# Three of four sums of weight halves moved from VectorE to GpSimd in a hybrid diffusion step

## The chip, the cores and the metric

The kernel runs on one core of a Trainium2 chip. A core has TensorE for matrix products (PE in the profile; PEld is its loading of weights), VectorE (DVE), ScalarE (ACT), GpSimd (POOL), and SyncE (SP), which starts DMA transfers. Each engine works through its own queue of instructions in order. The metric is the device time of one launch in microseconds. The kernel before was timed three times: 2074.26, 2075.63 and 2076.05 us, median 2075.63 us.

## The reference

One inference step through two layers, for 512 latent tokens and 128 context tokens (640 in all) with 1024 features, in float32:

```
h = RMSNorm(x) * (1 + scale1) + shift1            # modulation vectors: SiLU(cond) @ w_ada + b_ada
z = h @ w_in                                      # one projection for all branches, 6688 columns
A = gated linear attention (4 heads, both directions, chunks of 64)
B = short gated convolution;  C = Fourier mixing
x += gate1 * (sum_b sigmoid(G_b) * (branch_b @ W_b_out)) @ w_o
x += gate2 * (silu(g) * u) @ w_down,  with g, u = (RMSNorm(x) * (1 + scale2) + shift2) @ w_up
```

A final RMSNorm gives y_prompt and y_sample; the final attention states of the context are a third output.

## The kernel before

Features lie on the 128 partitions, tokens along the free axis, in two halves of 320 (256 latent and 64 context tokens). The products are made in float32 accuracy from two rounded parts: each operand is split into a high part (fp32r) and a low part, its difference from the high part, and three matmuls stand for one product (`mm3`, L224 to L226; `dense`, L242).

**Pairs of blocks.** Most of the projection (24 pairs of 128-column blocks in each layer, tiles `w1p_*`) and most of the up-projection (19 pairs in each layer, `wup_*`) are made two blocks at a time by the seven products of Strassen and Winograd (`pair`). That takes sums of halves of the weights and sums of the tokens' halves, and after the products four sums on the DVE that bring the seven results together in a tile `z`: L269, L271, L275 and L279, each with one operand in PSUM and one in SBUF. One pair has 84 matmuls of 320 columns.

**The weight stream.** Weights come by DMA into `raw` tiles (`_load`, six buffers; an SP transfer each). `_prep` turns them into chunks; a pair has four, called a, b, c and d. With r1 and r2 the two blocks' weights [128 x 1024] and a11, a12, a21, a22 their halves of 512 columns:

- chunk a is r1 itself;
- chunk b is `sb` = (a21 + a22 - a11, a11 - a21), with a21 + a22 kept as the first half of `sc`: L162, L163, L164;
- chunk c is `sc` = (a21 + a22, a12 - first half of `sb`): L168;
- chunk d is a22.

Each chunk is then split by `_split`: ScalarE copies it to `whi` (L140) and the DVE subtracts to get `wlo` (L141). `sb` and `sc` come from one pool with two buffers. `prefetch` prepares chunks up to two ahead of the one that TensorE takes.

**Around it.** In the mixer the heads of the attention run as generators beside the pairs: after certain products a step of the current head is issued (`tick_bg`). A head has, on the DVE, two scans (L617, L618), products with exponentials (L627 to L635), a serial chain of 14 small updates of the chunk states `S` (L667) and more; `S` shares its two buffers with the `z` tiles, and two memsets on GpSimd (L648, L649) clear parts of it. Modulation vectors (`ada`) come in between. In the feed-forward part the products down stand between the pairs up. GpSimd otherwise does a few transfers and memsets.

**The order.** The kernel is written in Tile: a planner lays out each engine's queue beforehand by priorities (the order of the program) and by its own idea of when operands and buffers are free, and puts in the waits. An engine's instructions can stand in another order than the program's text; on the chip an instruction that waits holds all behind it on its engine.

Of the kernel before, what the change touches and what calls it, by code (L numbers as in the profile page):

```python
# [16 lines left out]
PSUM = bass.MemoryType.PSUM  # L17
DRAM = bass.MemoryType.DRAM

P = 128  # L20
# [3 lines left out]
T = 640  # L24
TH = 320
# [21 lines left out]


def ffn_order():
    """The blocks of the second residual branch: those of one chunk's products down stand between the next's up."""  # L50
    todo = []
    for ci, (c0, n) in enumerate(FF_CHUNKS):
        for i in range(n):
            yield "up", ci, c0 + i
            for _ in range(-(-len(todo) // (n - i))):
                yield todo.pop(0)
        todo = [("down", ci, j) for j in range(KB)]


def ada_after(l, phase, i):  # L60
    """The quarters of modulation vectors made after the i-th block of a phase."""
    if phase == "mix":
        seq = [(l, v, n) for v in (G1, SH2, SC2, G2) for n in range(4)]
        return seq[i // 3 * 2 + i % 3 - 1:][:1] if i % 3 else []
    seq = [(1, v, n) for v in (SC1, SH1) for n in range(4)]
    return seq[i // 2 - 2:][:1] if l == 0 and i % 2 == 0 and 4 <= i < 20 else []
# [26 lines left out]
class Builder:  # L93
# [9 lines left out]
        self.n = 0  # L103
        self.gens, self.later, self.ada_last, self.last_act = [], [], None, None

# [1 line left out]
    def name(self, s):  # L107
        self.n += 1
        return f"{s}_{self.n}"
# [4 lines left out]
    def psum(self, s="ps"):  # L114
        return self.pp.tile([P, 1024], F32, tag="ps", name=self.name(s))

# [1 line left out]
    def start_stream(self, plan):  # L118
        self.plan = plan
        self.loads, self.chunks = [], []  # L120
# [23 lines left out]
    def _prep(self, c):  # L144
        nc = self.nc
        i, stage = self.chunks[c]
        if stage == "r":
            return
        if stage == "f":
            n = self.plan[i][2][0].shape[1]  # L150
            self.hl[c] = self._split(self.raw.pop((i, 0))[:, 0:n], n)
            self.freed += 1
            return
        r1, r2 = self.raw[i, 0], self.raw[i, 1]
        a11, a12, a21, a22 = r1[:, 0:512], r1[:, 512:1024], r2[:, 0:512], r2[:, 512:1024]
        if stage == "a":
            self.hl[c] = self._split(r1, 1024)
        elif stage == "b":
            sb = self.wp.tile([P, 1024], F32, tag="ws", name=self.name("sb"), bufs=2)
            sc = self.wp.tile([P, 1024], F32, tag="ws", name=self.name("sc"), bufs=2)  # L160
            self.sums[i] = sb, sc
            nc.vector.tensor_add(sc[:, 0:512], a21, a22)  # L162
            nc.vector.tensor_sub(sb[:, 0:512], sc[:, 0:512], a11)  # L163
            nc.vector.tensor_sub(sb[:, 512:1024], a11, a21)  # L164
            self.hl[c] = self._split(sb, 1024)
        elif stage == "c":
            sb, sc = self.sums.pop(i)
            nc.vector.tensor_sub(sc[:, 512:1024], a12, sb[:, 0:512])  # L168
            self.hl[c] = self._split(sc, 1024)
        else:  # L170
            self.hl[c] = self._split(a22, 512, True)
            del self.raw[i, 0], self.raw[i, 1]
            self.freed += 2
# [10 lines left out]
        return self.hl.pop(c)  # L184

    def prefetch(self, ahead):
        """Splits the weights that come next, up to some chunks ahead of the last taken."""
        self._load()
        while self.prepped < len(self.chunks):
            j = self.chunks[self.prepped][0]  # L190
            if sum(1 for q in range(self.used, self.prepped + 1) if self.chunks[q][1] != "d") > ahead:
                break
            if any((j, n) not in self.raw for n in range(len(self.plan[j][2]))):
                break
            self._prep(self.prepped)
            self.prepped += 1
            self._load()

# [1 line left out]
    def step(self, gens):  # L200
        for g in list(gens):
            try:
                next(g)
            except StopIteration:
                gens.remove(g)
# [12 lines left out]
        while self.gens:  # L218
            self.tick()

# [1 line left out]
    def mm3(self, o, lh, ll, rh, rl, start, stop):  # L222
        nc = self.nc
        nc.tensor.matmul(o, lh, rh, start=start, stop=False)  # L224
        nc.tensor.matmul(o, lh, rl, start=False, stop=False)  # L225
        nc.tensor.matmul(o, ll, rh, start=False, stop=stop)  # L226
# [16 lines left out]
        return ps  # L243

    def pair(self, key, h, T12, T34):
        """Two blocks of 128 columns over 8 blocks of the features and both halves of the tokens by the
        seven products of Strassen and Winograd; the two results, each [P, 2, TH]."""
        nc = self.nc

        def prod(o, w, c0, ops):  # L250
# [50 lines left out]
        self.nc.scalar.copy(hi, src)  # L301
        self.nc.vector.tensor_sub(lo, src, hi.bitcast(F32))

# [1 line left out]
    def consts(self):  # L305
        nc, cp, a = self.nc, self.cp, self.a
        self.ident = cp.tile([P, P], F32, name="ident")
# [27 lines left out]
            p["A2"] = cp.tile([P, KB, 2], F32, name=f"A2{l}")  # L335
            self.par.append(p)

# [1 line left out]
    def ada_mm(self, ps, kp, raw):  # L339
        r = raw.rearrange("p (k c) -> p k c", k=4)  # L340
        for j in range(4):
# [16 lines left out]
                nc.vector.scalar_tensor_tensor(p[A][:, ks], mv, 1.0, p[norm][:, ks], ALU.add, ALU.mult)  # L358

    def ada(self, pieces):  # L360
        """Quarters of modulation vectors; what follows the products comes one piece later."""
        for l, v, n in pieces:
            ps = self.psum("ada")
            for kp in range(2):
                self.ada_mm(ps, kp, self.take(("ada", l, v, n, kp)))
            self.ada_flush()
            self.ada_last = l, v, n, ps
# [3 lines left out]
            self.ada_end(*self.ada_last)  # L371
        self.ada_last = None

# [1 line left out]
    def table(self, name):  # L375
        """Loads a table set behind the functions of the one before."""
        self.in_order(lambda: self.tc.keep_in_program_order(self.nc.scalar.preload_act_table_set(name)))

    def act(self, *args, **kw):
        """A function that not all table sets have."""  # L380
        self.in_order(lambda: self.nc.scalar.activation(*args, **kw))  # L381

    def in_order(self, make):
# [40 lines left out]
        return r  # L424

    def modulate(self, half, r, xs, A, sh, out, hx):
        """Yields after each feature block's part of h."""
        nc = self.nc
        hs = slice(half * TH, half * TH + TH)

        def first(k):
            if len(hx) == k:
                hx.append(self.unit(s="hx"))
            nc.vector.tensor_mul(hx[k][:, hs], xs[k][:, hs], r)
            for i, (c0, n) in enumerate(((0, 256), (256, 64))):
                o = hx[k][:, half * TH + c0:half * TH + c0 + n]
                nc.scalar.activation(o, o, AF.Identity, scale=A[:, k, i:i + 1], bias=sh[:, k, i:i + 1])

        first(0)
        first(1)  # L440
        for k in range(KB):
            if k + 2 < KB:
                first(k + 2)
            if half == 0:
                out.append([])
            self.split_half(half, hx[k], out[k])
            yield
# [30 lines left out]
            self.nc.vector.scalar_tensor_tensor(o, ps[:, half * 512 + s:half * 512 + s + n], g[:, j, i:i + 1], o, ALU.mult, ALU.add)  # L478

    def boundary(self, keys, rhs, xs, g, after_x, norm, head, gk=None, tail=3):  # L480
        """The blocks that end a residual branch, the norm, and the blocks that start the next phase.

        The last few of the former and all of the latter go by halves of the tokens, so that the norm of
        one half runs beside the products of the other."""
        self.table("natural_log_exp_and_others")
        n = len(rhs)
        for j in range(KB - tail):
# [5 lines left out]
        last = range(KB - tail, KB)  # L493
# [50 lines left out]
            self.mm3h(ps, w, kb, self.hcur[kb], half, kb == 0, kb == KB - 1)  # L544

    def start(self, x, xs, A, sh, head):
        """The first norm and the first blocks, in the order in which the vectors come in."""
        nc = self.nc
        h, hx = [], []
        self.hcur, self.hx = h, hx  # L550
# [32 lines left out]
                    self.head_block(hps, hws, 0, k, half)  # L583
        return h, hx, hps

# [1 line left out]
    def to_tokens(self, u):  # L587
        """[P channels, T] to [P tokens, 5, P channels], in PSUM."""
        pt = self.psum("tt")
        for i in range(5):  # L590
            self.nc.tensor.transpose(pt[:, i * P:i * P + P], u[:, i * P:i * P + P], self.ident)
        return pt

# [1 line left out]
    def gla_start(self, l):  # L595
        nc = self.nc
        nc.gpsimd.tensor_scalar_mul(self.par[l]["nb_gk"], self.par[l]["b_gk"], -1.0)
# [99 lines left out]
        nc.vector.tensor_mul(yo, yo, r)  # L697
        yos[hd] = yo

# [1 line left out]
    def conv(self, l, j, sc, sx):  # L701
        nc = self.nc
        w = self.par[l]["conv_w"]
# [7 lines left out]
        nc.vector.scalar_tensor_tensor(cc[:, 4, 63:64], uc[:, 9, 0:1], w[:, 2, j:j + 1], cc[:, 4, 63:64], ALU.mult, ALU.add)  # L711
        return cv

# [1 line left out]
    def dft_load(self):  # L715
        out = []
        for i in range(2):
# [4 lines left out]
        return out  # L722

    def fourier(self, l, fxn, fr):
        """The Fourier mixing of both sequences. The even frequencies of the latent tokens come from the sums
        of the two halves of the positions, the odd ones from their differences."""
        nc = self.nc
        raw, d = self.dft_load(), []

# [82 lines left out]
            fr[g] = both(*u)  # L812
            yield

# [1 line left out]
    def make_plan(self):  # L816
        a = self.a
        plan = []
# [48 lines left out]
                full(("wd", l, ci, j), a["wd"][l, j][:, c0 * P:(c0 + n) * P])  # L867
        return plan

# [1 line left out]
    def gated(self, l, b, j, br, y, out):  # L871
        nc = self.nc
        nxt = BRANCHES.index(b) * KB + j + 2
# [198 lines left out]
    Builder(stack, tc, a).build()  # L1072


# [1 line left out]
def _blocks(w):  # L1076
    l, k, n = w.shape
    return np.ascontiguousarray(w.reshape(l, k // P, P, n // P, P).transpose(0, 3, 2, 1, 4).reshape(l, n // P, P, k))
# [80 lines left out]
```

## Time and profile before

| what | value |
|---|---|
| median of three runs | 2075.63 us |
| span of the profiled execution | 2075.0 us |
| TensorE busy | 2012.5 us, 97% |
| DVE busy | 1570.5 us, 76%, 2508 instructions |
| ScalarE busy | 919.4 us, 44% |
| GpSimd busy | 18.2 us, 1%, 52 instructions |
| mean granted clock of TensorE | 0.995 |

The profiled execution gives no time of its own beside its span; the span is 0.6 us below the median of the runs. A busy time counts the parts of the span in which an engine had an instruction under way. Matmuls are pipelined and overlap: one lasts some 0.31 us and the next starts 0.15 us later, so small gaps do not show in TensorE's busy time. The same holds on a smaller scale for the DVE, whose instructions start a little before the one ahead has ended.

### The profile page before, as it was taken

How to read it: one execution, taken by the hardware profiler on the slowest of the kernel's cores; microseconds unless marked ns; L12 is line 12 of the kernel's file. 1: busy time of each engine (PE TensorE's matmuls, PEld its weight loads, DVE VectorE, ACT ScalarE, POOL GpSimd, SP SyncE). 2: the span in 40 equal slices, each digit the busy share in tenths (PEclk: the TensorE clock that was granted, in tenths of full speed). 3: DMA queues.
4: the chain of work that ended last, by engine and by line, in shares of the span. 5: the costliest groups of instructions: out<-in, count | busy, mean ns of one | idle time of the engine just before them, and what ended most of it. 6: DMA issues, size and time to landing. Idle time of an engine off the chain costs nothing. (4 is left out here: it accounts for less than half of the span.)

```text
span 2075.0 us, 35216 instructions
## 1 busy us (share of the span) xinstructions
PE 2012.5 (97%) x14100; PEld 1936.3 (93%) x14100; DVE 1570.5 (76%) x2508; ACT 919.4 (44%) x1445; POOL 18.2 (1%) x52
## 2 busy tenths in 40 slices
PE   5999999999999999999999999999999999999997
PEld 2999998999999999999979999899999999999997
DVE  5778798877667777777677878898765787877876
ACT  5554435445445333333365454544543643333333
POOL 2000000000000000000000000000000000000000
PEclk9999999999999999999999999999999999999999
DMA  8254442554612333333232453335545222222222
GB/s 320 69 171 136 148 140 95 186 197 141 210 55 62 103 118 98 105 114 103 83 126 84 165 171 132 118 129 173 192 153 173 62 64 78 78 92 71 88 72 71
DMA packets 107139, 256.72 MB, mean 124 GB/s; under 512 B 13344, under 2 KB 46304, under 8 KB 106976
## 3 DMA queue, kind: packets, MB, share of 16 engines
q1 hardware_dynamic: 102528, 250.91, 36.8%
q8 instruction: 111, 1.82, 0.4%
q10 hardware_dynamic: 3728, 2.49, 0.4%
q0 software_dynamic: 720, 1.07, 0.1%
q14 instruction: 52, 0.43, 0.1%
HBM read 227.69 MB, written 26.74 MB: 123 GB/s over the span
## 5 line engine op out<-in xcount | busy, mean ns | idle before, releaser
L140 ACT CAST whi<-raw 128x1024 fp32r<-128x1024 f32 (+2 forms) x368 | 270.1, 734 | 529.5 <-PE wo L242 37.3
L141 DVE TENSOR_TENSOR wlo<-raw,whi 128x1024 fp32r<-128x1024 f32 (+2 forms) x368 | 304.4, 828 | 112.2 <-ACT whi L140 111.8
L242 PE MATMUL wd<-ffhi,whi 128*128 128x320 f32 x656 | 150.2, 310 | 0.0
L242 PE MATMUL wd<-fflo,whi 128*128 128x320 f32 x656 | 149.5, 309 | 0.0
L242 PE MATMUL wd<-ffhi,wlo 128*128 128x320 f32 x656 | 149.4, 309 | 0.0
L140 ACT CAST whi<-sb 128x1024 fp32r<-128x1024 f32 x86 | 90.3, 1050 | 125.7 <-PE wd L242 31.5
L140 ACT CAST whi<-sc 128x1024 fp32r<-128x1024 f32 x86 | 90.3, 1050 | 107.8 <-PE wd L242 48.0
L141 DVE TENSOR_TENSOR wlo<-sc,whi 128x1024 fp32r<-128x1024 f32 x86 | 104.9, 1220 | 30.2 <-ACT whi L140 29.6
L473 DVE SCALAR_TENSOR_TENSOR x<-wd,mod,x 128x512 f32<-128x512 f32 x212 | 106.7, 545 | 23.0 <-PE wd L242 23.0
L242 PEld LDWEIGHTS wd<-ffhi,whi 128*128 128x128 f32 x656 | 109.4, 188 | 3.3 <-ACT whi L140 3.3
L141 DVE TENSOR_TENSOR wlo<-sb,whi 128x1024 fp32r<-128x1024 f32 x86 | 104.8, 1219 | 6.8 <-ACT whi L140 6.7
L242 PEld LDWEIGHTS wd<-ffhi,wlo 128*128 128x128 f32 x656 | 109.7, 188 | 0.0
L242 PEld LDWEIGHTS wd<-fflo,whi 128*128 128x128 f32 x656 | 109.6, 188 | 0.0
L162 DVE TENSOR_TENSOR sc<-raw 128x512 f32<-128x512 f32 x86 | 59.3, 689 | 27.3 <-DMA raw<-in_w 26.0
L342 PE MATMUL ada<-raw,cond 128*32 128x256 f32 x768 | 56.5, 410 | 9.2 <-ACT cond L381 5.5
L163 DVE TENSOR_TENSOR sb<-sc,raw 128x512 f32<-128x512 f32 x86 | 59.1, 687 | 0.5
L168 DVE TENSOR_TENSOR sc<-raw,sb 128x512 f32<-128x512 f32 x86 | 59.1, 687 | 0.3
L242 PE MATMUL wb<-bhi,whi 128*128 128x320 f32 x256 | 59.2, 312 | 0.0
L164 DVE TENSOR_TENSOR sb<-raw,raw 128x512 f32<-128x512 f32 x86 | 59.0, 686 | 0.0
L242 PE MATMUL wb<-bhi,wlo 128*128 128x320 f32 x256 | 58.4, 309 | 0.0
L242 PE MATMUL wb<-blo,whi 128*128 128x320 f32 x256 | 58.3, 309 | 0.0
L342 PEld LDWEIGHTS ada<-raw,cond 128*32 128x32 f32 x768 | 20.8, 114 | 31.7 <-issue 7.2
(2254 smaller groups left out, 6417.0 us busy)
## 6 DMA issues: line engine op xcount, KB each, us to landing
raw<-in_w SPq DMA_DIRECT2D x104, 512.0 KB, 4.4
raw<-in_w_ada SPq DMA_DIRECT2D x96, 512.0 KB, 3.8
raw<-in_wu SPq DMA_DIRECT2D x88, 512.0 KB, 3.6
raw<-in_wd SPq DMA_DIRECT2D x96, 192.0 KB, 2.3
sgd<-z SPq DMA_DIRECT2D x48, 320.0 KB, 3.1
sgl<-sgd SPq DMA_DIRECT2D x48, 320.0 KB, 3.8
raw<-in_wb SPq DMA_DIRECT2D x48, 256.0 KB, 2.8
raw<-in_wo SPq DMA_DIRECT2D x16, 512.0 KB, 3.5
```

The source lines that it names most:

```text
L140: self.nc.scalar.copy(hi[:, 0:n], src)
L141: self.nc.vector.tensor_sub(lo[:, 0:n], src, hi[:, 0:n].bitcast(F32))
L162: nc.vector.tensor_add(sc[:, 0:512], a21, a22)
L163: nc.vector.tensor_sub(sb[:, 0:512], sc[:, 0:512], a11)
L164: nc.vector.tensor_sub(sb[:, 512:1024], a11, a21)
L168: nc.vector.tensor_sub(sc[:, 512:1024], a12, sb[:, 0:512])
L242: nc.tensor.matmul(o[h], w[:, sl], rhs[kb][h][part], start=(kb == 0 and first), stop=(kb == nk - 1 and last))
L342: self.nc.tensor.matmul(ps[32 * j:32 * j + 32, 0:256], self.cond[:, 4 * kp + j, :], r[:, j, :], start=(kp == 0), stop=(kp == 1))
L473: self.nc.vector.scalar_tensor_tensor(seg(xv), seg(v), g[:, j, i:i + 1], seg(xv), ALU.mult, ALU.add)
```

## The change

Three of the four sums are issued on GpSimd instead of the DVE: a21 + a22 and a11 - a21 of chunk b, and the second half of chunk c. The sum at L163 and all splits stay on the DVE. What is computed stays the same, operation for operation.

```
             self.sums[i] = sb, sc
-            nc.vector.tensor_add(sc[:, 0:512], a21, a22)
+            nc.gpsimd.tensor_add(sc[:, 0:512], a21, a22)
             nc.vector.tensor_sub(sb[:, 0:512], sc[:, 0:512], a11)
-            nc.vector.tensor_sub(sb[:, 512:1024], a11, a21)
+            nc.gpsimd.tensor_sub(sb[:, 512:1024], a11, a21)
             self.hl[c] = self._split(sb, 1024)
         elif stage == "c":
             sb, sc = self.sums.pop(i)
-            nc.vector.tensor_sub(sc[:, 512:1024], a12, sb[:, 0:512])
+            nc.gpsimd.tensor_sub(sc[:, 512:1024], a12, sb[:, 0:512])
             self.hl[c] = self._split(sc, 1024)
```

The rest of the diff takes out comments and docstrings; the line numbers stay.

## Rows read from the trace of the kernel before

**Rows 1.** The page: its first part (busy time of each engine, share of the span, instructions) and the DVE's line of its second part (busy share in tenths, 40 slices of 51.9 us).

```profile
PE 2012.5 (97%) x14100; PEld 1936.3 (93%) x14100; DVE 1570.5 (76%) x2508; ACT 919.4 (44%) x1445; POOL 18.2 (1%) x52
...
DVE  5778798877667777777677878898765787877876
```

**Rows 2.** Busy time of each engine in four stretches: the two mixers (70 to 470 us and 1085 to 1470 us) and the two feed-forward parts (680 to 1050 us and 1690 to 2045 us). Columns: the stretch, its length, then busy us and number of instructions of PE, PEld, DVE, ACT and POOL, the granted clock of TensorE, the share of the DMA engines, GB/s.

```profile
70.00:470.00 400.00, 392.09 (x2840) 372.41 (x2839) 324.80 (x503) 191.85 (x297) 3.66 (x13) 0.99 0.43 144
...
680.00:1050.00 370.00, 370.00 (x2592) 363.74 (x2591) 273.87 (x426) 132.37 (x189) 0.00 (x0) 1.00 0.34 109
...
1085.00:1470.00 385.00, 375.27 (x2738) 355.61 (x2740) 319.64 (x493) 186.61 (x284) 3.67 (x13) 1.00 0.43 142
...
1690.00:2045.00 355.00, 355.00 (x2423) 355.00 (x2422) 269.40 (x397) 127.86 (x178) 0.00 (x0) 1.00 0.26 78
```

**Rows 3.** What TensorE's matmuls waited for, over the whole span: the waiting tile and line, the releaser, total us, times, longest. L279 is the DVE's last sum of a pair of blocks.

```profile
PE w1p_17a L224 <- DVE z L279: 4.1, 2, 2.3
...
PE w1p_36a L224 <- DVE z L279: 2.9, 2, 1.5
...
PE w1p_44b L224 <- DVE z L279: 2.0, 2, 1.6
...
PE w1p_10a L224 <- DVE z L279: 0.5, 2, 0.3
```

**Rows 4.** The page's groups of instructions: two of the four sums, and the low part of the chunk that two of them feed. Columns: busy us, mean ns of one, then the DVE's idle time before them and what ended it.

```profile
L162 DVE TENSOR_TENSOR sc<-raw 128x512 f32<-128x512 f32 x86 | 59.3, 689 | 27.3 <-DMA raw<-in_w 26.0
...
L163 DVE TENSOR_TENSOR sb<-sc,raw 128x512 f32<-128x512 f32 x86 | 59.1, 687 | 0.5
...
L141 DVE TENSOR_TENSOR wlo<-sb,whi 128x1024 fp32r<-128x1024 f32 x86 | 104.8, 1219 | 6.8 <-ACT whi L140 6.7
```

**Rows 5.** The DVE's instructions in order of time in a crowded stretch of the second mixer: start us, duration us, line, tiles, shapes.

```profile
1275.89 0.69 DVE L162 TENSOR_TENSOR sc<-raw 128x512 f32<-128x512 f32 x1 [2.67 <-DMA raw<-in_w]
1276.50 0.68 DVE L164 TENSOR_TENSOR sb<-raw,raw 128x512 f32<-128x512 f32 x1
1277.10 0.68 DVE L163 TENSOR_TENSOR sb<-sc,raw 128x512 f32<-128x512 f32 x1
1277.71 0.83 DVE L616 TENSOR_TENSOR u<-u,u 128x640 f32<-128x640 f32 x1
```

**Rows 6.** GpSimd's groups of instructions: its widest write, the only two that read a tile, and the memsets of the state tile S with what ended GpSimd's idle time.

```profile
L603 POOL MEMSET zb<- 128x640 f32 x2 | 1.3, 640 | 1.7 <-DVE t L293 1.7
...
L597 POOL TENSOR_SCALAR nb_gk<-b_gk 128x4 f32<-128x4 f32 x2 | 0.5, 236 | 2.8 <-DMA b_gk<-in_b_gk 2.8
...
masks.py:199 POOL TENSOR_SCALAR_AFFINE_SELECT ident<-ident 128x128 f32<-128x128 f32 x1 | 0.3, 309 | 0.1
...
L648 POOL MEMSET S<- 64x128 f32 x8 | 1.6, 199 | 529.9 <-DVE wlo L141 192.7 <-DMA sgd<-z 137.2 <-DVE sb L163 71.6
```

**Rows 7.** In order of time, one memset on GpSimd and two of the DVE's sums beside it (start us, duration us).

```profile
1101.05 0.64 POOL L599 MEMSET scanm<- 128x640 f32 x1 [751.13 <-DVE tlo L302]
...
1101.17 0.49 DVE L291 TENSOR_TENSOR t<-hx,hx 128x320 f32<-128x320 f32 x1
1101.57 0.49 DVE L292 TENSOR_TENSOR t<-hx,t 128x320 f32<-128x320 f32 x1
```

**Rows 8.** Busy time of the DVE in the second mixer (1085 to 1470 us) by source line, in this order: L162, L164, L168, L269, L271, L275, L279. Columns: the stretch, its length, busy us and number of instructions.

```profile
1085.00:1470.00 385.00, 15.87 (x23) 1.00 0.43 142
...
1085.00:1470.00 385.00, 15.78 (x23) 1.00 0.43 142
...
1085.00:1470.00 385.00, 15.80 (x23) 1.00 0.43 142
...
1085.00:1470.00 385.00, 19.66 (x24) 1.00 0.43 142
...
1085.00:1470.00 385.00, 11.72 (x24) 1.00 0.43 142
...
1085.00:1470.00 385.00, 19.70 (x24) 1.00 0.43 142
...
1085.00:1470.00 385.00, 19.42 (x24) 1.00 0.43 142
```

**Rows 9.** The DVE's instructions in order of time ahead of a wait of TensorE in the second mixer.

```profile
1176.87 0.68 DVE L168 TENSOR_TENSOR sc<-raw,sb 128x512 f32<-128x512 f32 x1
...
1179.40 0.69 DVE L162 TENSOR_TENSOR sc<-raw 128x512 f32<-128x512 f32 x1
...
1180.01 1.93 DVE L667 SCALAR_TENSOR_TENSOR S<-S,g 64x128 f32<-64x128 f32 x5
...
1183.23 2.63 DVE L667 SCALAR_TENSOR_TENSOR S<-S,g 64x128 f32<-64x128 f32 x7
...
1185.90 1.23 DVE L141 TENSOR_TENSOR wlo<-sc,whi 128x1024 fp32r<-128x1024 f32 x1
...
1187.54 0.82 DVE L279 TENSOR_TENSOR z<-w1p_34d,z 128x640 f32<-128x640 f32 x1
```

**Rows 10.** Two stretches of 25 us of the first mixer; columns as in rows 2.

```profile
275.00:300.00 25.00, 22.73 (x172) 21.44 (x171) 22.03 (x38) 9.55 (x19) 0.40 (x2) 0.93 0.40 137
...
325.00:350.00 25.00, 23.10 (x157) 22.08 (x156) 24.04 (x39) 9.31 (x16) 0.40 (x2) 0.93 0.22 63
```

## The prediction, made before the result was known

> **What bounds the kernel now.** I read the page's busy times first. TensorE is busy in 97% of the span, the DVE in 76%, GpSimd in 1% [rows 1]. Of the 2075.0 us only 62.5 are free of matmuls, so nothing that is done to the DVE can bring more than part of that. The busy times by stretch say where the free time lies [rows 2]: in the two feed-forward parts TensorE is busy in 370.00 of 370 us and in 355.00 of 355 us, so there the DVE, at 274 and 269 us, costs nothing. In the two mixers TensorE is free for 400 - 392.1 = 7.9 us and 385 - 375.3 = 9.7 us, 17.6 us together, while the DVE is busy for 81% and 83%. The other 45 us lie at the start, at the two ends of residual branches and at the end, where no pair is made. The list of waits names the releaser in the mixers [rows 3]: TensorE waits for the DVE's last sum of a pair (L279) for 4.1 + 2.9 + 2.0 + 0.5 = 9.5 us, in eight places, four in each layer. These 9.5 us are what a lighter DVE can win and what a heavier one makes larger.
>
> How such a wait comes about is seen in order of time [rows 9]: between 1176.87 and 1188.36 us the DVE has two of the sums, the chain of 14 updates of S, splits, and only then the L279 that frees the PSUM tile. The whole queue is late, not one instruction.
>
> **What is removed.** One of the sums lasts 0.69 us [rows 4], but in a crowded stretch the next starts 0.60 us after it (1275.89, 1276.50, 1277.10, 1277.71) [rows 5]. So a pair gives back 3 x 0.60 = 1.8 us of the DVE's queue; over 86 pairs that is 155 us. In the second mixer's stretch there are 23 such sums of each kind [rows 8], so 23 x 1.8 = 41 us of 385.
>
> **What is added.** GpSimd gets the same three instructions for each pair. The trace has no sum of two tiles on GpSimd. Bounds of its duration at 512 columns: from below the widest memset, 640 ns for 640 columns, scaled to 0.51 us; from above the one operation over a whole tile that reads a tile, 309 ns for 128 columns [rows 6], times four for the columns and twice for the second operand, 2.5 us. I take 4 x 0.309 = 1.24 us, as the nearest row reads, computes and writes. Then GpSimd is busy for 23 x 3 x 1.24 = 86 us of 385, and with the upper bound for 170 us: it does not become the bound by its own time.
>
> **What GpSimd costs the DVE** is the term that decides. From below: nothing. Beside a memset at 1101.05 the DVE's sums at 1101.17 and 1101.57 last 0.49 us each and keep their 0.40 us spacing [rows 7]; but a memset reads nothing. From above: the DVE stands still for the whole of each GpSimd sum, 86 us against the 41 removed. I take the middle case, that only those DVE instructions stand still that read two operands from SBUF, as GpSimd's sums do, and that instructions with an operand in PSUM go on. In the second mixer the DVE has 319.6 us [rows 2]; less the three sums (15.87 + 15.78 + 15.80 = 47.5) and the four sums behind the products (19.66 + 11.72 + 19.70 + 19.42 = 70.5) [rows 8] that leaves 201.7 us, 52% of 385. A GpSimd sum that falls anywhere then costs the DVE 0.52 x 1.24 = 0.65 us, and 69 of them cost 45 us, against 41 us removed. The DVE gains nothing and loses nothing. With 0.51 us for one the DVE gains 41 - 18 = 23 us, with 2.5 us it loses 90 - 41 = 49 us of the 65 us that it is free now; both ends stay in the range.
>
> The Trainium skill has a rule for this ("SBUF — State Buffer", section "Who interferes with whom"): a DVE instruction with two inputs in SBUF contends with a GpSimd instruction that reads SBUF, not with one that only writes, and whichever comes second waits until the first is done. The memset row agrees with its second half, and no run here yet shows the first. Without the rule, by the memset row alone, the sum would be the first rival's 2066 us; by the rule it is the 52% above.
>
> The Trainium skill also prices such a sum ("GPSIMD Engine Reference", section "Performance versus the Vector engine"): 1.96 times the DVE's time for the same sum. On the DVE's 0.69 us that is an estimate of 1.35 us, by which the 45 us would be 48 us; the sum of the forecast would not move.
>
> **What moves in the queues.** The sum that stays (L163) now waits at the head of the DVE's queue for GpSimd's first sum. Behind it stand splits and the sums after the products, so a late GpSimd would hold all of them, and then TensorE. But the first sum needs only the raw weights and a free buffer, and GpSimd's queue has nothing else than a few memsets, so it starts as soon as it may, often long before the DVE reaches L163: L162 stands at 1179.40, ahead of the chain of S [rows 9]. The wait for weights that the DVE had at L162, 26 us in all [rows 4], moves to GpSimd, and to L163 behind it. Where weights come that late, L163 ends 1.24 + 0.60 us after them and the three sums ended 1.8 us after them: equal. ScalarE's copy of `sb` waits for GpSimd's second sum in the same way. In GpSimd's queue the memsets of S (L648) wait for a buffer that a transfer or the DVE must free [rows 6]; sums behind such a memset wait too. No transfer is issued on another queue than before; SP's loads keep their order. The planner lays out the queues anew for the lighter DVE; which instruction goes ahead of which there can move single waits of 1 to 2 us either way.
>
> **The sum.** Feed-forward parts: nothing, because TensorE has no gap there to fill, and even the upper case (18 pairs x 3 x 1.24 - 18 x 1.8 = +35 us on 274) leaves the DVE at 309 of 370 us. Mixers: the DVE's load stays the same, so the 9.5 us of waits stay. Span 2075.0 + 0; with the 0.6 us that the median lies above the profiled span, 2075.6, I say 2075.5 us. Its own range is 2072 to 2079, for the waits that a new order shifts.
>
> **Rivals.**
>
> 1. *GpSimd's sums cost the DVE nothing, and the waits go.* Then each of the eight waits is shortened by up to the 1.8 us that leave the queue ahead of it. The two at w1p_17a (up to 2.3) lose 1.8 each, the two at w1p_36a their 2.9 us, those at w1p_44b and w1p_10a their 2.5 us: 9.0 us, 2066 us. Two stretches of the first mixer have a mean granted clock of 0.93 after such waits [rows 10]; if those dips went too, 2 x 0.07 x 25 = 3.5 us more. Range 2062 to 2071. For it speaks that the waits are the DVE's own; against it that GpSimd's sums, unlike its memsets, read two tiles.
>
> 2. *The DVE is held where it is already late: slower.* In the stretch ahead of a wait [rows 9] the queue holds the chain of S (64 partitions, two operands in SBUF) and splits, hardly anything with PSUM. Two GpSimd sums become free to run there, as the splits release their buffers, and each holds the DVE for the whole of its 1.24 us: 2.5 us against the 1.2 us of L168 and L162 that leave. Each of the eight heads' waits grows by 1.3 us, 10 us in all: 2086 us, and with dips of the clock as in rows 10 behind longer waits up to 2096. It decides as soon as the held share there is over 1.2 / 2.5 = 48%, if nothing else makes room. Against it: six of the fifteen slices that lie in the mixers have the DVE at 7 tenths [rows 1], so it can recover between heads.
>
> 3. *GpSimd is late.* Memsets of S that wait, or sums that themselves wait for the DVE, make L163 stand at the head of the DVE's queue for up to one GpSimd sum. With one such wait of 1.24 us for each of four heads in a layer that reaches TensorE, half of it hidden: 8 x 0.6 = 5 us, 2080 us.
>
> 4. *The change doesn't do what it says*, for instance if GpSimd refused to run beside the DVE at all: the DVE's 86 - 41 = +45 us in each mixer would leave it 92 to 95% busy there; the time is that of rival 2 at its upper end.
>
> **How the numbers follow.** A measurement of this kernel can tell 0.2%, 4.2 us, from no change: 2071.5 to 2079.8. I give the forecast 0.40, the first rival 0.32, the second with the fourth 0.20, the third 0.08. Most of the forecast's cases lie within 0.2%, and a few of the first rival's smallest gains fall there too, against a few of the forecast's that leave it: same 0.39, faster 0.32, slower 0.29 (0.20 + 0.05 of the third and 0.04 of the forecast's upper edge). The range for 8 in 10 reaches to the first rival's lower part and to the second's middle: 2063 to 2088.
>
> **What would show it.** In the profile after: the duration of L162, L164 and L168 on GpSimd (1.24 us; over 2 or under 0.8 moves the sum); the mean of the DVE's L141 and L163, which now stand at 1.22 and 0.69 us: longer if GpSimd holds the DVE, unchanged if not; L279 beside it should not lengthen. The DVE's busy time in 1085 to 1470 us: about 320 by the forecast, 278 by the first rival, over 335 by the second. TensorE's waits for L279: 9.5 us by the forecast, under 2 by the first rival, near 20 by the second. A wait of L163 for GpSimd in the DVE's list, over 20 us, would be the third. The forecast is wrong if TensorE's free time in the mixers leaves 14 to 21 us, or if the feed-forward parts change at all.

## The result, and the profile after

The changed kernel takes 2105.25 us (median of four runs, 2104.44 to 2107.64) against 2075.84 us of the kernel before beside it. The ratio is 1.0146, with a 95% interval of 1.0132 to 1.0160: slower by 1.5%, some 30 us. The forecast was 2075.5 us with a range of 2063 to 2088. The profiled execution has a span of 2103.3 us, 28.3 us more than before. One execution each of e3 and e5 below (2814 and 2202 us) ran at a much lower granted clock, 0.66 and 0.85, and is left out of their medians and ratios.

First the page of the changed kernel: the busy times, and the groups of the sums and of one split (columns as in [rows 4]).

```profile
PE 2024.4 (96%) x14100; PEld 1947.7 (93%) x14100; DVE 1544.0 (73%) x2250; ACT 919.2 (44%) x1445; POOL 410.3 (20%) x310
...
L162 POOL TENSOR_TENSOR sc<-raw 128x512 f32<-128x512 f32 x86 | 122.0, 1419 | 1335.1 <-DVE wlo L141 533.7
...
L164 POOL TENSOR_TENSOR sb<-raw,raw 128x512 f32<-128x512 f32 x86 | 128.5, 1494 | 177.0 <-DVE wlo L141 168.9
...
L168 POOL TENSOR_TENSOR sc<-raw,sb 128x512 f32<-128x512 f32 x86 | 143.1, 1664 | 96.9 <-DVE sb L163 96.3
...
L163 DVE TENSOR_TENSOR sb<-sc,raw 128x512 f32<-128x512 f32 x86 | 120.7, 1403 | 49.5 <-POOL sc L162 46.9
...
L141 DVE TENSOR_TENSOR wlo<-sc,whi 128x1024 fp32r<-128x1024 f32 x86 | 113.1, 1315 | 36.0 <-ACT whi L140 35.7
```

The DVE has 258 instructions less, but its busy time falls only from 1570.5 to 1544.0 us. The three sums that left were worth 3 x 59 = 177 us of it by their own durations and about 155 us by their spacing. The rest is found again as longer durations: L163, untouched by the change, goes from 0.687 [rows 4] to 1.403 us, 62 us over the 86 pairs, and the split of `sc` from 1.220 to 1.315 us; smaller amounts lie in other splits and in the DVE's work for the heads and the convolution. The sums behind the products, which have one operand in PSUM (where the matmuls put their results; the other tiles lie in SBUF), are not longer: the second mixer's 24 of L269 take 19.56 us against 19.66 before [rows 8]. On GpSimd a sum takes 1.42 to 1.66 us in the mean; the shortest of them take 1.26 us.

Where the 28.3 us lie: the next rows cover, for each kernel, the pairs of the two mixers, from the first pair's first product to the last pair's d product (columns as in [rows 2]; in the second mixer both ends are 1.3 us later within those products). Before:

```profile
78.20:447.10 368.90, 360.99 (x2615) 342.11 (x2614) 303.98 (x468) 176.40 (x269) 3.66 (x13) 0.99 0.43 143
...
1098.90:1467.00 368.10, 358.37 (x2616) 339.15 (x2615) 305.51 (x470) 176.17 (x269) 3.67 (x13) 1.00 0.43 144
```

After:

```profile
77.50:456.40 378.90, 364.31 (x2617) 344.75 (x2616) 296.25 (x402) 176.76 (x269) 110.48 (x81) 0.98 0.42 139
...
1112.20:1492.70 380.50, 364.18 (x2616) 344.69 (x2615) 299.90 (x403) 176.71 (x270) 109.95 (x81) 0.98 0.42 139
```

The two stretches grow by 10.0 and 12.4 us. TensorE's free time in them goes from 7.9 + 9.7 = 17.6 to 14.6 + 16.3 = 30.9 us, +13.3 us. The other 9.1 us are in its busy time, with 2615 to 2617 matmuls in each of the four: the granted clock falls from 0.99 and 1.00 to 0.98 in both. In stretches of 25 us, those with a mean granted clock of 0.93 were two, both in the first mixer [rows 10]; now there are eight in the two mixers, two of which are:

```profile
1300.00:1325.00 25.00, 23.00 (x156) 21.95 (x156) 22.03 (x29) 9.03 (x14) 9.22 (x6) 0.93 0.47 157
...
1400.00:1425.00 25.00, 24.73 (x186) 23.64 (x187) 20.77 (x41) 8.43 (x18) 6.18 (x4) 0.93 0.42 146
```

Each such stretch has 7% of 25 us, 1.75 us, less of the full clock, so six more of them account for 10.5 us, near the 9.1. Note the DVE: it is *less* busy than before in these stretches (296.2 and 299.9 against 304.0 and 305.5 us).

The feed-forward parts, which [rows 2] showed without a gap, still have none:

```profile
667.00:1030.00 363.00, 363.00 (x2544) 356.75 (x2544) 266.59 (x367) 130.60 (x188) 73.79 (x53) 1.00 0.32 100
...
1704.00:2055.00 351.00, 351.00 (x2396) 351.00 (x2395) 259.33 (x345) 126.21 (x177) 76.92 (x53) 1.00 0.27 81
```

Of the remaining 5.9 us, 5.4 are at the ends of the first residual branches, where the first pairs of the feed-forward part are prepared: from the first matmul of `wo` to the first pair it takes 107.1 instead of 104.2 us and 106.8 instead of 104.3 us. TensorE's busy time has 1.6 and 1.2 us of that, in stretches where the granted clock is lower than before (0.98 against 1.00).

What TensorE waited for after, the largest that the DVE's sums of a pair release (against the four rows of [rows 3]):

```profile
PE u L653 <- DVE z L269: 8.1, 4, 2.7
...
PE w1p_48d L224 <- DVE z L269: 4.2, 2, 2.2
...
PE w1p_36a L224 <- DVE z L279: 3.4, 2, 2.3
...
PE w1p_40d L224 <- DVE z L269: 2.5, 2, 1.3
...
PE w1p_44b L224 <- DVE z L279: 2.3, 2, 1.9
...
PE w1p_17a L224 <- DVE z L279: 1.3, 2, 0.7
```

L279 is still there with 3.4 + 2.3 + 1.3 us, but most is now L269, the *first* sum of a pair, which stood in no such row before. (`u` is a product of an attention head; it needs the PSUM tile that L269 frees.) In the DVE's own queue, L163 waits for GpSimd:

```profile
DVE sb L163 <- POOL sc L162: 46.9, 16, 5.8
```

The order of time at one late pair of the first mixer shows both together. Before, on the DVE:

```profile
151.77 0.69 DVE L162 TENSOR_TENSOR sc<-raw 128x512 f32<-128x512 f32 x1 [3.66 <-DMA raw<-in_w]
...
152.98 0.69 DVE L163 TENSOR_TENSOR sb<-sc,raw 128x512 f32<-128x512 f32 x1
...
153.58 1.22 DVE L141 TENSOR_TENSOR wlo<-raw,whi 128x1024 fp32r<-128x1024 f32 x1
...
154.71 0.82 DVE L269 TENSOR_TENSOR z<-w1p_34b,s 128x640 f32<-128x640 f32 x1
```

After, GpSimd, then the DVE, then TensorE and the clock of TensorE just behind (columns as in [rows 2]):

```profile
152.94 1.30 POOL L162 TENSOR_TENSOR sc<-raw 128x512 f32<-128x512 f32 x1 [11.26 <-DMA raw<-in_w]
...
154.20 1.29 POOL L164 TENSOR_TENSOR sb<-raw,raw 128x512 f32<-128x512 f32 x1
...
156.12 2.18 POOL L168 TENSOR_TENSOR sc<-raw,sb 128x512 f32<-128x512 f32 x1 [0.63 <-DVE sb L163]
```

```profile
154.27 1.77 DVE L163 TENSOR_TENSOR sb<-sc,raw 128x512 f32<-128x512 f32 x1 [5.75 <-POOL sc L162]
...
155.96 1.21 DVE L141 TENSOR_TENSOR wlo<-raw,whi 128x1024 fp32r<-128x1024 f32 x1
...
157.10 0.81 DVE L269 TENSOR_TENSOR z<-w1p_34b,s 128x640 f32<-128x640 f32 x1
```

```profile
157.97 1.53 PE L653 MATMUL u<-v,koT 64*128 64x128 f32 x18 [1.88 <-DVE z L269]
```

```profile
159.20:162.40 3.20, 3.20 (x13) 2.98 (x12) 2.99 (x6) 2.45 (x10) 1.27 (x1) 0.50 0.45 164
```

Before, the first sum starts when the weights are there (151.77) and L269 starts 2.94 us later. After, GpSimd starts its first sum at 152.94. L163 waits for it until 154.27, and in the same moment GpSimd starts its second sum (154.20). L163 lasts 1.77 us instead of 0.69: it ends when the second sum has ended (155.49) and its own 0.6 us are over. L269 starts 4.16 us after the first sum did, 1.2 us later than before. The third sum at 156.12 lasts 2.18 us: this time the DVE's split (155.96 to 157.17) was first. TensorE waits 1.88 us for L269, where before it went through the same products without a wait, and behind the wait the granted clock is 0.50, the lower of its two levels (1.2 instead of 2.4 GHz). Late weights are not the reason in general: measured against the matmuls at the same place of TensorE's queue, the 104 loads of `w_in` land 0.3 us earlier than before in the mean.

The smallest example is an instruction of four columns. Beside a GpSimd sum from 115.22 to 116.52, the DVE's sum L355 (0.16 us on its own) lasts until just that end:

```profile
115.22 1.30 POOL L162 TENSOR_TENSOR sc<-raw 128x512 f32<-128x512 f32 x1
```

```profile
115.56 0.97 DVE L355 TENSOR_TENSOR mod<-mod,b_ada 128x4 f32<-128x4 f32 x1
```

### The profile page after: what moved, and what is told of

It reads as the page before. It is cut to its first block, busy times and chain, and to the rows that moved or that the text cites. A ratio compares the mean times of both kernels' runs of the same rounds, so it can differ in the third digit from the quotient of the medians.

```text
span 2103.3 us, 35457 instructions
## 1 busy us (share of the span) xinstructions
PE 2024.4 (96%) x14100; PEld 1947.7 (93%) x14100; DVE 1544.0 (73%) x2250; ACT 919.2 (44%) x1445; POOL 410.3 (20%) x310
## 5 line engine op out<-in xcount | busy, mean ns | idle before, releaser
L141 DVE TENSOR_TENSOR wlo<-raw,whi 128x1024 fp32r<-128x1024 f32 (+2 forms) x368 | 323.9, 881 | 120.7 <-ACT whi L140 120.1
L162 POOL TENSOR_TENSOR sc<-raw 128x512 f32<-128x512 f32 x86 | 122.0, 1419 | 1335.1 <-DVE wlo L141 533.7
L164 POOL TENSOR_TENSOR sb<-raw,raw 128x512 f32<-128x512 f32 x86 | 128.5, 1494 | 177.0 <-DVE wlo L141 168.9
L168 POOL TENSOR_TENSOR sc<-raw,sb 128x512 f32<-128x512 f32 x86 | 143.1, 1664 | 96.9 <-DVE sb L163 96.3
L163 DVE TENSOR_TENSOR sb<-sc,raw 128x512 f32<-128x512 f32 x86 | 120.7, 1403 | 49.5 <-POOL sc L162 46.9
L140 ACT CAST whi<-sc 128x1024 fp32r<-128x1024 f32 x86 | 90.3, 1050 | 136.4 <-PE wd L242 48.0
L141 DVE TENSOR_TENSOR wlo<-sc,whi 128x1024 fp32r<-128x1024 f32 x86 | 113.1, 1315 | 36.0 <-ACT whi L140 35.7
```

The lines of the kernel that those rows point to most:

```text
L140: self.nc.scalar.copy(hi[:, 0:n], src)
L141: self.nc.vector.tensor_sub(lo[:, 0:n], src, hi[:, 0:n].bitcast(F32))
L162: nc.gpsimd.tensor_add(sc[:, 0:512], a21, a22)
L164: nc.gpsimd.tensor_sub(sb[:, 512:1024], a11, a21)
L168: nc.gpsimd.tensor_sub(sc[:, 512:1024], a12, sb[:, 0:512])
```

## The experiments

Three theories stood against each other. **Held**: a GpSimd instruction that reads SBUF stops the DVE's instructions with two operands in SBUF for its whole length. **Wait**: the cost is the DVE's new wait at L163 for a slower engine. **Order**: the cost is the planner's new order of the queues. Ratios below are each against runs of the kernel before on the same chip, with 95% intervals.

**Nothing read (e1).**

```
-            nc.gpsimd.tensor_add(sc[:, 0:512], a21, a22)
+            nc.gpsimd.memset(sc[:, 0:512], 0.01)
...
-            nc.gpsimd.tensor_sub(sb[:, 512:1024], a11, a21)
+            nc.gpsimd.memset(sb[:, 512:1024], 0.01)
...
-            nc.gpsimd.tensor_sub(sc[:, 512:1024], a12, sb[:, 0:512])
+            nc.gpsimd.memset(sc[:, 512:1024], 0.01)
```

> The three sums on GpSimd are replaced by memsets of the same three tile halves, so these sums are left out and the output is not the reference's. Same engine, same wait of L163 for GpSimd, but nothing read from SBUF. Theory 'held' (a GpSimd instruction that reads SBUF stops the DVE's two-operand instructions for its whole length): L163 back to 0.69 us, L141 at its old means, TensorE free for under 12 us in the two mixers, 2062 to 2070 us. Theory 'order' (the planner's new queues cost the time): above 2090 us. Theory 'wait' (L163 waiting for another engine costs the time): 2080 us or more.

2061.77 us, ratio 0.9931 (0.9916 to 0.9945): 14 us faster than before. Busy times, two groups of the DVE and one of GpSimd:

```profile
PE 2006.6 (97%) x14100; PEld 1933.5 (94%) x14100; DVE 1423.8 (69%) x2250; ACT 920.0 (45%) x1445; POOL 148.2 (7%) x310
...
L163 DVE TENSOR_TENSOR sb<-sc,raw 128x512 f32<-128x512 f32 x86 | 59.2, 688 | 3.1
...
L141 DVE TENSOR_TENSOR wlo<-sc,whi 128x1024 fp32r<-128x1024 f32 x86 | 105.0, 1220 | 44.9 <-ACT whi L140 44.5
...
L162 POOL MEMSET sc<- 128x512 f32 x86 | 45.3, 526 | 1531.8 <-DVE wlo L141 1483.3 <-DVE mod L355 48.5
```

Every duration of the DVE in these groups is back at its old value, and its busy time falls by 147 us, near the 155 us that the forecast set for the three sums. TensorE is free for 10.1 us in the mixers (4.6 + 5.4), under the 12 expected. The DVE's queue in the mixers stands in the changed kernel's order but for single neighbours that swap. So the planner's order is not the cause: nearly the same queues run in 2062 us if GpSimd only writes. But a memset needs no weights and is done early, so the wait of L163 did not stay as expected: the DVE's list has none for GpSimd. This run takes away the reading and the lateness together, and shows what the first rival would have been worth; the next one parts them.

**The wait kept, nothing read (e9).**

```
-            nc.gpsimd.tensor_add(sc[:, 0:512], a21, a22)
-            nc.vector.tensor_sub(sb[:, 0:512], sc[:, 0:512], a11)
-            nc.gpsimd.tensor_sub(sb[:, 512:1024], a11, a21)
+            for t in (a21, a21, a21): nc.gpsimd.memset(t, 0.01)
+            nc.vector.tensor_sub(sb[:, 0:512], a21, a11)
+            for t in (sb[:, 512:1024], sb[:, 512:1024], sc[:, 0:512]): nc.gpsimd.memset(t, 0.01)
...
-            nc.gpsimd.tensor_sub(sc[:, 512:1024], a12, sb[:, 0:512])
+            for _ in range(3): nc.gpsimd.memset(sc[:, 512:1024], 0.01)
```

> Each of the three sums on GpSimd is replaced by three memsets of 512 columns, some 1.4 us as long as a sum; the first three write over a21, so they wait until the weights have landed, and L163 reads a21 and so waits for them. The sums are left out. GpSimd's wait for the weights, its length and the DVE's wait for it at L163 are as with the change; only the reading of SBUF is gone. Theory 'held': no DVE instruction lengthens; 2062 to 2072 us. Theory 'wait' (GpSimd's latency ahead of L163 costs the time): 2085 us or more, with L163's wait at 40 us or more.

2070.43 us, ratio 0.9979 (0.9968 to 0.9991). The wait of L163 is as long as with the change, the durations of these groups are those of before, and the pairs of the mixers look like this:

```profile
DVE sb L163 <- POOL raw L162: 49.4, 30, 5.8
```

```profile
L163 DVE TENSOR_TENSOR sb<-raw,raw 128x512 f32<-128x512 f32 x86 | 59.3, 689 | 51.2 <-POOL raw L162 49.4
...
L141 DVE TENSOR_TENSOR wlo<-sc,whi 128x1024 fp32r<-128x1024 f32 x86 | 104.8, 1219 | 34.3 <-ACT whi L140 33.9
```

```profile
76.20:440.00 363.80, 357.28 (x2617) 338.96 (x2616) 264.98 (x400) 176.49 (x269) 106.41 (x214) 1.00 0.44 145
...
1092.90:1462.10 369.20, 359.90 (x2616) 340.43 (x2616) 267.17 (x401) 175.92 (x269) 106.35 (x214) 1.00 0.42 143
```

A late GpSimd in front of L163 therefore costs 8.7 us against e1 (2070.43 - 2061.77; 10 by the ratios), from the waiting that it puts at the head of the DVE's queue; it does not make the kernel slower than before. The queues of this kernel are not in the changed kernel's order, so this 8.7 us is good to a few us only. Memsets do hold some DVE instructions, small copies with a single operand: the 32 casts of L455 go from 0.325 to 0.363 us in the mean, the longest lasts 0.84 us, and with the copies of L625 and L626 that is 3 us in all.

**Reading added, nothing taken away (e10).** The kernel before, whose DVE queue keeps its order instruction for instruction, with sums on GpSimd that nobody needs (line breaks added here):

```
             nc.vector.tensor_add(sc[:, 0:512], a21, a22)
+            gs = self.wp.tile([P, 240], F32, tag="gs", name=self.name("gs"), bufs=1)
+            [nc.gpsimd.tensor_tensor(gs, u[:, s:s + 240], v[:, s:s + 240], ALU.add)
+             for s in (0, 240) for u, v in ((a21, a22), (a11, a21))]
...
             nc.vector.tensor_sub(sc[:, 512:1024], a12, sb[:, 0:512])
+            gs = self.wp.tile([P, 240], F32, tag="gs", name=self.name("gs"), bufs=1)
+            [nc.gpsimd.tensor_tensor(gs, a12[:, s:s + 240], a11[:, s:s + 240], ALU.add)
+             for s in (0, 240)]
```

> The kernel before, its DVE queue in the same order, with six GpSimd sums of 240 columns added per pair, of the same halves, into a tile that nobody reads. No instruction of the DVE waits for GpSimd by a semaphore (raw buffers come free a little later). Theory 'held': the DVE's two-operand instructions lengthen by over 100 us in all; nothing was taken from it, so the time is above the change's: 2105 to 2130 us. Theory 'wait': 2073 to 2080 us.

2140.48 us, ratio 1.0319 (1.0302 to 1.0337): 66 us slower, above the range expected. Busy times, two groups of the DVE, then the mixers:

```profile
PE 2039.8 (95%) x14100; PEld 1954.8 (91%) x14100; DVE 1729.8 (81%) x2508; ACT 918.3 (43%) x1445; POOL 590.8 (28%) x568
...
L141 DVE TENSOR_TENSOR wlo<-sc,whi 128x1024 fp32r<-128x1024 f32 x86 | 118.0, 1372 | 19.8 <-ACT whi L140 19.3
...
L163 DVE TENSOR_TENSOR sb<-sc,raw 128x512 f32<-128x512 f32 x86 | 77.4, 900 | 0.5
```

```profile
78.50:476.20 397.70, 372.11 (x2617) 349.33 (x2616) 345.56 (x472) 176.99 (x271) 142.27 (x139) 0.97 0.40 132
...
1134.30:1531.10 396.80, 369.36 (x2616) 346.32 (x2615) 346.83 (x474) 177.04 (x271) 142.36 (x140) 0.98 0.41 133
```

The DVE's busy time rises by 159 us (1729.8 against 1570.5) though it does the same work in the same order and waits for GpSimd by no semaphore. Nor are the weights later, though GpSimd reads `raw` too and so could keep its buffers: the DVE's first sums wait for them 23.4 us in all, against 26.0 us before.

```profile
DVE sc L162 <- DMA raw<-in_w: 23.4, 9, 3.9
```

TensorE's free time in the pairs of the mixers grows to 25.6 + 27.4 us. This is the held theory by itself. The condition of two operands in SBUF shows here too: the second mixer's 24 of L269, with one operand in PSUM, take 19.54 us.

**Parts of the change.** Only one or two of the three sums stay on GpSimd. First L164 and L168 (e2):

```
-            nc.gpsimd.tensor_add(sc[:, 0:512], a21, a22)
+            nc.vector.tensor_add(sc[:, 0:512], a21, a22)
```

> The sum that L163 needs (L162) is back on the DVE; the other two stay on GpSimd. Theory 'wait': L163 waits for nobody, time back to 2073 to 2079 us. Theory 'held': two of three holds remain, L163 no longer collides each time, 2083 to 2095 us. Theory 'order': anywhere in 2075 to 2100 us.

2085.19 us, ratio 1.0049 (1.0034 to 1.0064). L163 waits for nobody now, and the loss is still a third of the change's; L163 is held by GpSimd's second sum:

```profile
L163 DVE TENSOR_TENSOR sb<-sc,raw 128x512 f32<-128x512 f32 x86 | 90.6, 1053 | 1.7
```

Only L164 on GpSimd (e3):

```
-            nc.gpsimd.tensor_add(sc[:, 0:512], a21, a22)
+            nc.vector.tensor_add(sc[:, 0:512], a21, a22)
...
-            nc.gpsimd.tensor_sub(sc[:, 512:1024], a12, sb[:, 0:512])
+            nc.vector.tensor_sub(sc[:, 512:1024], a12, sb[:, 0:512])
```

> Only a11 - a21 (L164) on GpSimd. Theory 'wait': no wait of the DVE for GpSimd, 2073 to 2078 us. Theory 'held': one hold per pair against 0.6 us removed, 2078 to 2086 us.

2081.73 us (1.0030, 1.0020 to 1.0040). Held beats wait here: no DVE instruction waits for GpSimd, and it is slower than before.

Only L162 (e5):

```
-            nc.gpsimd.tensor_sub(sb[:, 512:1024], a11, a21)
+            nc.vector.tensor_sub(sb[:, 512:1024], a11, a21)
...
-            nc.gpsimd.tensor_sub(sc[:, 512:1024], a12, sb[:, 0:512])
+            nc.vector.tensor_sub(sc[:, 512:1024], a12, sb[:, 0:512])
```

> Only a21 + a22 (L162) on GpSimd, so only the sum that L163 waits for. Theory 'wait': most of the +29 us is here, 2095 to 2105 us. Theory 'held': one hold per pair, 2080 to 2090 us.

2086.42 us (1.0055, 1.0038 to 1.0072), within the held theory's 2080 to 2090. The wait at L163 is small when GpSimd has only this sum to do:

```profile
DVE sb L163 <- POOL sc L162: 17.2, 15, 1.2
```

Only L168 (e6):

```
-            nc.gpsimd.tensor_add(sc[:, 0:512], a21, a22)
+            nc.vector.tensor_add(sc[:, 0:512], a21, a22)
...
-            nc.gpsimd.tensor_sub(sb[:, 512:1024], a11, a21)
+            nc.vector.tensor_sub(sb[:, 512:1024], a11, a21)
```

> Only a12 - first half of sb (L168) on GpSimd. No DVE instruction waits for it except the split of chunk c through ScalarE's copy. Theory 'wait': 2073 to 2078 us. Theory 'held': 2078 to 2086 us.

2075.48 us (1.0008, 0.9998 to 1.0017): no difference that can be told, in the wait theory's range and below the held theory's. The third sum follows L163, and in this kernel its holds fall on others: the split of 384 columns, which belongs to the feed-forward products, goes from 0.554 to 0.746 us in the mean, the splits of 1024 columns of `raw` from 1.221 to 1.296 us and L164 from 0.686 to 0.743 us, while L163 stays at 0.69 us and the splits of `sb` and `sc` at 1.22 us. One sum of 0.60 us for each of 86 pairs left the DVE, 52 us, and its busy time falls by only 5.2 us (1565.3 against 1570.5), so 47 us of holds, 26 of them in the mixers by the same count, leave the time as it was: TensorE is free for 15.5 us in the mixers against 17.6 before. So a hold costs what it delays, not its length. The three parts alone (e5, e3, e6) cost 11.4, 6.2 and 1.7 us by their ratios, 19 us together, against 30 for the change: together they cost more than apart. L163 lasts 1.05 us in the mean with the second sum alone and 1.40 us in the change, where it also starts late behind the first; that this makes up the difference is likely, but no run shows it.

**The other order on GpSimd (e4).**

```
+            nc.gpsimd.tensor_sub(sb[:, 512:1024], a11, a21)
             nc.gpsimd.tensor_add(sc[:, 0:512], a21, a22)
             nc.vector.tensor_sub(sb[:, 0:512], sc[:, 0:512], a11)
-            nc.gpsimd.tensor_sub(sb[:, 512:1024], a11, a21)
```

> As the change, but GpSimd makes a11 - a21 first and a21 + a22 second, so that no GpSimd sum stands ready to start beside L163. Theory 'held': mean of L163 from 1.40 to under 0.9 us; its wait grows by up to 1.3 us where the weights come late; 2095 to 2107 us, near the change's 2105. Theory 'wait': the longer wait shows, 2110 us or more.

2108.19 us (1.0158, 1.0141 to 1.0175). The sum that stayed on the DVE (here it is line 164) is never held, but what it gains it loses by waiting:

```profile
L164 DVE TENSOR_TENSOR sb<-sc,raw 128x512 f32<-128x512 f32 x86 | 59.2, 688 | 117.2 <-POOL sc L163 117.2
```

```profile
DVE sb L164 <- POOL sc L163: 117.2, 55, 6.9
```

It has 0.69 us back, and waits 117 instead of 47 us. The collision beside L163 and the wait in front of it are two ends of one rope: GpSimd needs 2 x 1.3 us for the two sums of chunk b, and the DVE's one sum between them is either behind one or beside one. The total lies between the two theories' ranges and decides nothing by itself. Nor does the DVE's busy time order these runs: here it is 1489.6 us, 81 us less than before, and the kernel is 33 us slower.

**By part of the network.** The three sums on GpSimd for the pairs of the mixers alone (e7), or for those of the feed-forward parts alone (e8, with `"wup"` in the first line):

```
+        e = nc.gpsimd if self.plan[i][0][0] == "w1p" else nc.vector
...
-            nc.gpsimd.tensor_add(sc[:, 0:512], a21, a22)
+            e.tensor_add(sc[:, 0:512], a21, a22)
...
-            nc.gpsimd.tensor_sub(sb[:, 512:1024], a11, a21)
+            e.tensor_sub(sb[:, 512:1024], a11, a21)
...
-            nc.gpsimd.tensor_sub(sc[:, 512:1024], a12, sb[:, 0:512])
+            e.tensor_sub(sc[:, 512:1024], a12, sb[:, 0:512])
```

> The change for the 48 pairs of the mixers alone. Segments of the two traces give +22.4 us to the mixers' pairs and +6 us to the ends of residual branches, whose first chunks are pairs of the next stage: 2096 to 2102 us by every theory.

2099.31 us (1.0120, 1.0105 to 1.0135). The pairs of the mixers in its profiled execution, of 2093.9 us, with the DVE's queue there in the changed kernel's order:

```profile
75.50:454.90 379.40, 361.10 (x2615) 341.57 (x2615) 298.30 (x402) 176.85 (x269) 110.86 (x81) 0.99 0.42 139
...
1108.40:1485.90 377.50, 361.30 (x2615) 341.77 (x2615) 298.18 (x403) 176.68 (x270) 110.28 (x81) 0.99 0.43 140
```

They lose nearly as much as the changed kernel's, 19.9 us against 22.4, with only four stretches at a clock of 0.93 in place of its eight: 16.9 us are free time of TensorE and 3.0 us busy time. So the loss is much the same in these two executions, but how it splits between waits and clock is not.

> The change for the 38 pairs of the feed-forward parts alone. TensorE has no gap there before or after; only the first pairs, prepared beside the norm between the branches, can cost: 2076 to 2082 us by every theory, with the DVE's holds as long as in the mixers.

2079.66 us (1.0027, 1.0018 to 1.0037). Both as expected; 25 + 6 us are the change's 30 within the runs' spread. In e8 the feed-forward parts themselves stay without a gap, and the first pairs behind `wo` come 3.5 and 2.7 us later than before.

## Why the prediction was wrong

- *What bounds the kernel*: right in the main. 22.4 of the 28.3 us are in the mixers, nothing is in the pairs of the feed-forward parts, and more than half of the loss is free time of TensorE, behind waits for the DVE. But the ends of the first residual branches, which the prediction put at nothing since no pair is made there, cost 5.4 us: the first pairs' chunks are prepared there, and e8 loses 6 us at these places.
- *What is removed*, 1.8 us of the DVE for a pair: right. e1 frees 147 us of the 155.
- *What is added*, 1.24 us for a GpSimd sum: right for an undisturbed one (1.26 to 1.30 us), with some luck, as it was scaled from one row of another operation; the mean of 1.42 to 1.66 has waiting for the DVE in it.
- *What GpSimd costs the DVE*: its size was right to a quarter, 45 us given back against 41 removed in a mixer. In the second mixer's stretch the DVE has 470 - 403 = 67 instructions less, 67 x 0.60 = 40 us, and its busy time fell by 305.5 - 299.9 = 5.6 us, so some 35 us were given back. That instructions are held for the whole of a GpSimd sum, and that those with an operand in PSUM go on, was an assumption; L355 bears out the first, L269 the second, and e1 and e10 that reading is the cause. The holds did not fall as evenly as the 52% had it: over the whole span some 128 of the 155 us removed came back, about half of them on L163. The rule of the Trainium skill that the prediction weighed ("SBUF — State Buffer", section "Who interferes with whom") agrees with these runs in both halves: memsets hold no instruction with two operands in SBUF (L163 at 0.688 us in e1, 0.689 in e9), sums that read hold even a four-column instruction (0.97 us).
- *The sum*: here it failed. "Mixers: the DVE's load stays the same, so the 9.5 us of waits stay." The load did stay the same, even a little under it; the waits did not. The sums of chunk b become ready together when a pair's weights come, and the DVE's work just behind them is that pair's L163, a split and L269, which TensorE waits for. So the holds sit where they cost most, and TensorE's free time in the mixers became 30.9 us instead of the 17.6 that were to stay. e6 is the counterpart: 52 us removed, 47 given back elsewhere, and the time stays, as the forecast had it for the whole.
- *What moves in the queues*: also wrong in a step. L163 was to end 1.24 + 0.60 us after late weights, the same as the three sums before. It ends 3.1 us after GpSimd's first sum starts (152.94 to 156.04), since GpSimd's second sum holds it. The wait was seen, not what starts beside the waiting instruction.
- *Rivals*: the second (held, slower, 2086 us and up to 2096) had the right cause at another place: not at the chain of S (L667 goes from 0.347 to 0.404 us in the mean, 6 us in all) but at L163 and L269 behind it. The third (GpSimd late, 2080) happened as well, and the two add up: by ratios to the kernel before, e1 is at -14 us, e9 at -4, the change at +30. So of the 44 us between a lighter DVE that is left alone and the change, about 10 go with lateness and about 34 with reading; as e9's queues have another order, that split is rough. The first rival's gain is there when nothing is read, 14 us instead of 9.
- *The clock*: the sum had nothing for it; the first rival named 3.5 us of dips that might go, the second more of them behind longer waits. In the changed kernel's profiled execution TensorE's busy time grew by 9.1 us in the mixers and 2.9 us at the ends of the branches, 12 of the 28.3 us; in the mixers of e7 it was 3.0 of 19.9.

What stays open: how the reading's 34 us split between holds of L163 and holds of other instructions; e4 shows that they cannot be taken away one by one. That a different order by hand (the second sum held back until L163 is done) would help was not tried.

No run of these that computes the whole is faster than the kernel before: e6 is level with it, and e1 and e9 leave sums out.

## What to carry to other kernels

An engine's work that moves to GpSimd is not off the DVE if both read SBUF: count the GpSimd instruction's whole length against the DVE's two-operand instructions beside it, and look which DVE instruction stands next to it, because operands that become ready together put the hold in front of the very chain that is already late. Equal load does not mean equal waits: before a load is traded for another, follow one late chain in order of time with both durations written in. And try such a move first with instructions that only write in place of those that read; the two runs together tell what the relief is worth and what the contention takes.

## What was not expected of the hardware

Idle GpSimd sums that no instruction waits for cost 66 us (e10), more than twice the change. In that kernel GpSimd's 240-column sums last 0.71 us undisturbed and 1.11 us in the mean, some 200 us more over 516 sums by the profile's rough spans of GpSimd, so the DVE holds GpSimd as well. And part of the loss, 12 of 28.3 us in the changed kernel's profiled execution, is not TensorE's waits but its lower granted clock behind them.
